# Low halves of 46 weight tiles: an accumulating DMA onto a negated copy in place of a VectorE subtraction

## The chip, the cores and the metric

The kernel runs on one core of one Trainium2 chip. The metric is device microseconds of one execution, lower being better. Three runs of the kernel before are shown (860.07, 862.01 and 861.69 us); their median is 861.69 us.

Engines are named as the profile names them: PE is TensorE (its weight loads are PEld), DVE is VectorE, ACT is ScalarE, POOL is GpSimd, and SP is the engine whose queue issues the kernel's DMAs.

## What is computed

One layer on a sequence of 512 rows of width 1024: a modulated standardisation, a mixer of two branches (an mLSTM with 4 heads and an S5 state-space branch with 32 groups), a layer norm, and a convolutional GLU feed-forward net with a hidden width of 2816. What matters here is the mixer, since the weights that the change touches are those of its input projection, its GLU and its down projection:

```python
proj = h @ w_in + b_in
xm, om, ip, fp, us, ga, gb = jnp.split(proj, IN_SPLITS, axis=-1)
...
y_a = (hm * mlstm_norm_gain * jax.nn.sigmoid(om)) @ w_mlstm_down
ys = jax.nn.gelu(_s5_ssm(us, ...))
val, gate = jnp.split(ys @ w_s5_glu, 2, axis=-1)
y_b = val * jax.nn.sigmoid(gate)
y = jax.nn.sigmoid(ga) * y_a + jax.nn.sigmoid(gb) * y_b
return y @ w_mix_out
```

All of it is float32. PE multiplies in the type float32r, which keeps fewer bits, so the kernel splits each operand into a high part (rounded to float32r) and a low part (what rounding left), and adds three products: high times high, high times low, low times high.

## The kernel before

Everything is tiled to 128 partitions. A weight tile `w` is 128 x 1024 float32 (512 KB): the eight 128 x 128 blocks that one output tile of 128 columns needs for its eight steps over the width of 1024. The SP queue loads it into one of two buffers `w`. ACT writes its rounded copy `wh` and DVE the difference `wl`, each into one of three buffers (`split_into`, L220 to L222; the DVE instruction stands on L210, in `sub`). PE then runs 8 times three matmuls of 512 columns (`mm3`, L241 to L244): L242 and L243 use `wh`, L244 uses `wl`.

46 such tiles go through a list, `todo` (L740 to L750): 30 of the input projection (`in_win`: the tiles x2 to x7, the eight o tiles and the sixteen g tiles), 8 of the GLU (`in_wglu`) and 8 of the down projection (`in_wdn`). `ahead` (L752) keeps a tile's pair one tile ahead of its use: with `PF = 1`, the split of tile i+1 is issued before the matmuls of tile i. With three buffers, the ACT copy of tile i+1 has to wait until PE has finished with tile i-2.

The order of the work is written by hand in the string `SEQ` (L144): tokens for the projection tiles (x, o, g), for steps of the S5 branch (S) and of the heads (H), for GLU and down tiles (l, d), and for steps of a second modulation product (A), which streams 256 KB pieces of `in_wa` through buffers `hh` and adds them up on DVE (L202, `s5h<-hh,k,s5h`). A scheduler of the framework then orders each engine's instructions by its own estimate, so that matmuls of projection tiles fill PE between the steps of heads and S5. In time, the kernel falls into these stretches: start and the eight k steps (the first of the 46 tiles is split at 57 us), projection tiles between heads and S5 (to 305 us; 26 of the 46 are split there), gate, GLU and down tiles back to back (305 to 428 us; the other 20, with A steps beside them), mix output and layer norm (428 to some 500 us), and the feed-forward net to the end.

POOL does small things: masks of the heads (`affine_select`, L854), the scaling of the o tiles (L786), inverse square roots (L278, L279), memsets. It issues no DMA.

Of the kernel before, what the change touches and what calls it, by code (L numbers as in the profile page):

```python
# [10 lines left out]
F32R = mybir.dt.float32r  # L11
I32 = mybir.dt.int32
AF = mybir.ActivationFunctionType
ALU = mybir.AluOpType
# [144 lines left out]
def _build(ctx, tc, nc, h):  # L159
    V, A, T, GP = nc.vector, nc.scalar, nc.tensor, nc.gpsimd  # L160
# [4 lines left out]
    def tl(tag, shape, dt=F32, bufs=None, pool=None):  # L165
        uid[0] += 1
        return (pool or sb).tile(list(shape), dt, tag=tag, name=f"{tag}_{uid[0]}", bufs=bufs or BUFS[tag])
# [11 lines left out]
    def big(shape=(P, D), dt=F32, tag="hb"):  # L179
        return tl(tag, shape, dt)  # L180
# [10 lines left out]
    def dma(o, i):  # L191
        return nc.sync.dma_start(o, i)  # L192
# [16 lines left out]
    def sub(o, a, b):  # L209
        V.tensor_tensor(o, a, b, op=ALU.subtract)  # L210

    def f32(ap):
        return ap.bitcast(F32)

    def wload(ap, n=D, tag="w"):
        w = big(tag=tag)
        dma(w[:, :n], ap)
        return w

    def split_into(hi, lo, x):  # L220
        A.copy(hi, x)  # L221
        sub(lo, x, f32(hi))  # L222

    def wsplit(ap, n=D, tags=("wh", "wl"), w=None):
        w = wload(ap, n) if w is None else w
        wh, wl = (big(dt=F32R, tag=t) for t in tags)
        split_into(wh[:, :n], wl[:, :n], w[:, :n])
        return wh, wl

    def new_pair(tag):  # L230
# [494 lines left out]
    def kstep(j):  # L725
        wc = nxt[1]
        if j < KD - 1:
            nxt[:] = wa_load(j + 1), w0_load(j + 1)
        w0h, w0l = wsplit(None, NXM0 * P, w=wc)
        if j < KD - 1:  # L730
            pend = ada1_mm(j + 1, nxt[0])
        for m in range(NXM0):
            if j < KD - 1 and m == M1:
                ada1_cols(j + 1, *pend)
            if j < KD - 1 and m == M2:
                htr(j + 1)
            sl = slice(m * P, (m + 1) * P)
            mm3(acc0[m], w0h[:, sl], w0l[:, sl], hp[j][0], hp[j][1], j == 0, j == KD - 1)

    todo, ready = [], []  # L740
# [10 lines left out]

    def ahead():  # L752
        while todo and len(ready) <= PF:
            ready.append(wsplit(todo.pop(0)))
        return ready.pop(0)

    def proj(m):
        if m < NXM0:
            return acc0[m]
        wh, wl = ahead()  # L760
        o = acc()
        for k in range(KD):
            sl = slice(k * P, (k + 1) * P)
            mm3(o, wh[:, sl], wl[:, sl], hp[k][0], hp[k][1], k == 0, k == KD - 1)
        return o
# [187 lines left out]
    def glu_tile(j):  # L953
        wh, wl = ahead()
        pvl, pgt = bank("hd"), bank("hd")
        for i, o in ((1, pgt), (0, pvl)):
            for k in range(4):
                sl = slice((4 * i + k) * P, (4 * i + k + 1) * P)
                mm3(o, wh[:, sl], wl[:, sl], ys[k][0], ys[k][1], k == 0, k == 3)
        b = hh()  # L960
        A.activation(b, pgt, AF.Tanh, scale=0.25)
        stt(b, b, 1.0, pvl, ALU.add, ALU.mult)
        stt(gab[j][:, 1], gab[j][:, 1], 1.0, b, ALU.add, ALU.mult)

    def down_tile(j):
        wh, wl = ahead()
        pa = acc()
        for k in range(KD):
            sl = slice(k * P, (k + 1) * P)
            mm3(pa, wh[:, sl], wl[:, sl], hmg[k][0], hmg[k][1], k == 0, k == KD - 1)  # L970
        a = hh()
        stt(a, gab[j][:, 0], 1.0, pa, ALU.add, ALU.mult)
        stt(a, gab[j][:, 1], 0.5, a)
        yp.append(pair_of(a, "hb" if j < 5 else "s5b" if j < 7 else "s5h"))
# [218 lines left out]
    def val_half(j, gg, ov):  # L1193
        tt(gg, ov, gg)
        gp_.append(pair_of(gg, "hp" if j < 8 else "hb" if j < 13 else "s5b" if j < 15 else "hx" if j < 18 else "gab"))

    early = [(u, wsplit(h["wup"][u], tags=("wh", "wl") if i < 3 else ("hb", "hb")), bank("hd"))
             for i, u in enumerate((1, 0, 3, 2)[:NS])]
    for hv in range(2):
# [10 lines left out]
    for j in range(NF):  # L1210
# [5 lines left out]
        for u in (2 * j + 1, 2 * j):  # L1216
            if u in pre:
                ou[u] = pre[u]
            else:
                w = wsplit(h["wup"][u])  # L1220
# [36 lines left out]
```

## Time and profile before

| | |
|---|---|
| three runs | 860.07, 862.01, 861.69 us; median 861.69 |
| profiled execution: span from first to last instruction | 862.0 us |
| PE, PEld busy | 828.5 us (96%), 669.2 us (78%) |
| DVE busy | 607.1 us (70%) |
| ACT busy | 368.6 us (43%) |
| POOL busy | 98.0 us (11%) |
| mean granted TensorE clock | 0.994 |
| DMA | 105.94 MB, mean 123 GB/s; HBM read 101.01 MB |

The profiled execution has no other time than its span, which lies within the three runs and 0.3 us above their median. Busy times are sums over the whole span, and a stage's own limit has to be read in that stage. Matmuls overlap in the records (one of 512 columns is shown as 0.39 to 0.40 us, and the next begins some 0.23 us after it), so a PE that is busy throughout can still hide small bubbles; idle time of PE is certain, busy time is not all work.

### The profile page before, as it was taken

The page shows a single profiled execution, that of the slowest core. Times are in us where ns is not written, and L with a number is a line of the kernel's source. Part 1 is how long each engine was busy: PE and PEld are TensorE (multiplying, and loading weights), DVE is VectorE, ACT ScalarE, POOL GpSimd, SP SyncE. Part 2 cuts the span into 40 slices and gives each one's busy share as a digit, 9 for nine tenths or more (in the row PEclk, how much of TensorE's full clock was granted, in tenths as well). Part 3 has the DMA queues.
Part 4 walks back from the last instruction along what each step waited for, and adds up shares of the span by engine and source line. Part 5 has one row for each costly group of instructions (what it writes and reads, how often), then busy time and mean ns, then how long its engine had stood idle before and what let it go on. Part 6 is the DMA issues. An engine that isn't in the chain of part 4 may idle for free.

```text
span 862.0 us, 11353 instructions
## 1 busy us (share of the span) xinstructions
PE 828.5 (96%) x4106; PEld 669.2 (78%) x4106; DVE 607.1 (70%) x1144; ACT 368.6 (43%) x589; POOL 98.0 (11%) x255
## 2 busy tenths in 40 slices
PE   3999999999999999999999999999999999999996
PEld 1777868778777778888887988888888878888785
DVE  5557978788689774578978767556777675878144
ACT  4454573564556442232334555444444444333000
POOL 2781211122022100000002200000000000000000
PEclk9999999999999999999999999999999999999998
DMA  9832132122222233568655023224444232445011
GB/s 336 288 132 86 53 101 62 45 85 62 79 60 87 86 123 122 196 203 294 210 191 177 2 74 102 94 98 147 146 147 137 86 120 74 171 163 169 11 49 49
DMA packets 45415, 105.94 MB, mean 123 GB/s; under 512 B 13360, under 2 KB 14256, under 8 KB 45360
## 3 DMA queue, kind: packets, MB, share of 16 engines
q1 hardware_dynamic: 45360, 105.23, 36.0%
q8 instruction: 32, 0.52, 0.2%
q14 instruction: 23, 0.19, 0.1%
HBM read 101.01 MB, written 2.10 MB: 120 GB/s over the span
## 4 chain that ended last, share of the span: by engine, by line
PE 76%; DVE 11%; ACT 4%; DMA 4%; issue 2%; SPq 2%; POOL 0%; DVEq 0%; ACTq 0%; POOLq 0%
PE acc L242 11%; PE acc L243 11%; PE acc L244 11%; PE hd L242 11%; PE hd L243 11%; PE hd L244 11%; DVE hh L202 2%; SPq L192 2%; DVE s5h L207 1%; PE s L242 1%; PE s L244 1%; PE s L243 1%; DVE wl L210 1%; PE s L612 1%; DMA w<-in_wmix 1%
## 5 line engine op out<-in xcount | busy, mean ns | idle before, releaser
L221 ACT CAST wh<-w 128x1024 fp32r<-128x1024 f32 (+2 forms) x103 | 103.2, 1003 | 144.0 <-PE acc L243 111.5
L210 DVE TENSOR_TENSOR wl<-w,wh 128x1024 fp32r<-128x1024 f32 (+2 forms) x103 | 120.5, 1172 | 60.8 <-ACT wh L221 60.1
L242 PE MATMUL acc<-hp,wh 128*128 128x512 f32 x256 | 103.4, 405 | 0.5 <-ACT hx L785 0.5
L244 PE MATMUL acc<-hp,wl 128*128 128x512 f32 x256 | 102.1, 399 | 0.0
L243 PE MATMUL acc<-hp,wh 128*128 128x512 f32 x256 | 102.1, 399 | 0.0
L242 PE MATMUL hd<-s5b,wh 128*128 128x512 f32 (+1 forms) x168 | 63.4, 380 | 0.7 <-ACT s5b L1169 0.5
L243 PE MATMUL hd<-s5b,wh 128*128 128x512 f32 (+1 forms) x168 | 63.6, 379 | 0.2 <-DVE s5b L210 0.2
L244 PE MATMUL hd<-s5b,wl 128*128 128x512 f32 (+1 forms) x168 | 63.3, 378 | 0.0
L242 PEld LDWEIGHTS acc<-hp,wh 128*128 128x128 f32 x256 | 48.2, 189 | 14.7 <-issue 3.7
L202 DVE SCALAR_TENSOR_TENSOR hh<-hh,hh 128x512 f32<-128x512 f32 x52 | 35.9, 691 | 31.2 <-ACT hh L564 14.7
L244 PEld LDWEIGHTS acc<-hp,wl 128*128 128x128 f32 x256 | 48.4, 189 | 11.2 <-issue 0.4
L243 PEld LDWEIGHTS acc<-hp,wh 128*128 128x128 f32 x256 | 48.4, 189 | 10.8 <-issue 0.4
L202 DVE SCALAR_TENSOR_TENSOR s5h<-hh,k,s5h 128x512 f32<-128x512 f32 x56 | 39.3, 746 | 4.7 <-DMA hh<-in_wa 4.6
L242 PEld LDWEIGHTS hd<-s5b,wh 128*128 128x128 f32 x168 | 31.3, 188 | 7.6 <-ACT s5b L1169 0.8
L243 PEld LDWEIGHTS hd<-s5b,wh 128*128 128x128 f32 x168 | 31.7, 189 | 7.0 <-DVE s5b L210 0.6
L244 PEld LDWEIGHTS hd<-s5b,wl 128*128 128x128 f32 x168 | 31.6, 188 | 6.4
L202 DVE SCALAR_TENSOR_TENSOR hh<-hh,k,hh 128x512 f32<-128x512 f32 x44 | 33.0, 751 | 4.5 <-ACT hh L1186 3.6
L1024 POOL TENSOR_SCALAR mov<-mov 128x1 f32<-128x1 f32 x6 | 3.7, 624 | 276.2 <-ACT s L1023 159.6
L244 PE MATMUL acc<-hx,wl 128*128 128x512 f32 x84 | 33.1, 394 | 0.0
L242 PE MATMUL acc<-hx,wh 128*128 128x512 f32 x84 | 33.1, 394 | 0.0
L243 PE MATMUL acc<-hx,wh 128*128 128x512 f32 x84 | 33.1, 394 | 0.0
L244 PE MATMUL acc<-s5b,wl 128*128 128x512 f32 x80 | 31.6, 395 | 0.5 <-DVE wl L210 0.5
(547 smaller groups left out, 2053.1 us busy)
## 6 DMA issues: line engine op xcount, KB each, us to landing
w<-in_wup SPq DMA_DIRECT2D x44, 512.0 KB, 3.2
hh<-in_wa SPq DMA_DIRECT2D x64, 256.0 KB, 4.2
w<-in_win SPq DMA_DIRECT2D x30, 512.0 KB, 3.2
w<-in_wfd SPq DMA_DIRECT2D x22, 512.0 KB, 3.3
hb<-in_wa SPq DMA_DIRECT2D x16, 512.0 KB, 7.4
w<-in_wglu SPq DMA_DIRECT2D x8, 512.0 KB, 3.3
w<-in_wdn SPq DMA_DIRECT2D x8, 512.0 KB, 3.3
w<-in_wmix SPq DMA_DIRECT2D x8, 512.0 KB, 4.2
```

The costliest lines, as they stand in the source:

```text
L192: return nc.sync.dma_start(o, i)
L202: V.scalar_tensor_tensor(o, i0, s, i1, op0=op0, op1=op1)
L207: V.tensor_tensor(o, a, b, op=op)
L210: V.tensor_tensor(o, a, b, op=ALU.subtract)
L221: A.copy(hi, x)
L242: T.matmul(o, lhsT=wh, rhs=xh, start=first, stop=False)
L243: T.matmul(o, lhsT=wh, rhs=xl, start=False, stop=False)
L244: T.matmul(o, lhsT=wl, rhs=xh, start=False, stop=last)
L612: T.matmul(o, lhsT=F[:, ri, pr, :], rhs=XB[:, ri, pr].rearrange("p g k -> p (g k)"), start=ri == 0, stop=False)
L1024: GP.tensor_scalar(v[:, 2:3], v[:, 0:1], v[:, 1:2], EPS * D, op0=ALU.add, op1=ALU.add)
```

## The change

For these 46 tiles DVE no longer subtracts. ACT still writes `wh`, and then writes minus `wh` into `wl`; POOL issues a DMA that reads the same 512 KB of the weight from HBM a second time and adds it, in flight, to what stands in `wl`. The sum is w minus wh, the same low half. The SP load of `w` stays, since `wh` is made from it. Buffers and `PF` are as before. The other splits (the first 8 steps' weights, the mix, feed-forward up and down weights, all activations) still go through DVE.

```diff
@@ -227,6 +227,14 @@
         split_into(wh[:, :n], wl[:, :n], w[:, :n])
         return wh, wl
 
+    def wsplit_dma(ap):
+        w = wload(ap)
+        wh, wl = (big(dt=F32R, tag=t) for t in ("wh", "wl"))
+        A.copy(wh, w)
+        A.activation(wl, f32(wh), AF.Copy, scale=-1.0)
+        GP.dma_start(wl, ap, accum_op=ALU.add)
+        return wh, wl
+
     def new_pair(tag):
         if tag in ("hx", "hh", "s5h"):
             return tl(tag, [P, 516], F32R)[:, :512], tl(tag, [P, 516], F32R)[:, :512]
@@ -751,7 +759,7 @@
 
     def ahead():
         while todo and len(ready) <= PF:
-            ready.append(wsplit(todo.pop(0)))
+            ready.append(wsplit_dma(todo.pop(0)))
         return ready.pop(0)
 
     def proj(m):
```

Lines of the changed kernel below the new function are 8 higher (L795 becomes L803). The scheduler also moves instructions. Three places follow. Names are tile names with a running number, output before the arrow.

First, DVE between the end of head 0 and the S5 step that follows (L207 on `s5h` is the S5 rotation). Before:

```order
L210 TENSOR_TENSOR wl_1772<-w_1769,wh_1771 128x1024
L207 TENSOR_TENSOR hh_1740<-hd_1735,hx_1192 128x512
L207 TENSOR_TENSOR hh_1751<-hd_1746,hx_1451 128x512
L210 TENSOR_TENSOR wl_1818<-w_1815,wh_1817 128x1024
L210 TENSOR_TENSOR hx_1743<-hh_1740,hx_1742 128x512
L202 SCALAR_TENSOR_TENSOR hh_1757<-hx_1009,k_61,hh_1757 128x512
```

and now:

```order
L207 TENSOR_TENSOR hh_1749<-hd_1744,hx_1195 128x512
L207 TENSOR_TENSOR hh_1760<-hd_1755,hx_1456 128x512
L210 TENSOR_TENSOR hx_1752<-hh_1749,hx_1751 128x512
L202 SCALAR_TENSOR_TENSOR hh_1766<-hx_1011,k_61,hh_1766 128x512
L210 TENSOR_TENSOR hx_1763<-hh_1760,hx_1762 128x512
```

The two subtractions into `wl` are gone from between the head's own steps; the rest keeps its order.

Second, ACT among gate tiles of the stretch from 305 to 428 us (L795, now L803, evicts a gate tile from PSUM; L961, now L969, a GLU tile's). Before:

```order
L221 CAST wh_3629<-w_3627 128x1024
L795 ACTIVATE gab_3555<-acc_3562,k_95 128x512
L221 CAST wh_3671<-w_3669 128x1024
L795 ACTIVATE gab_3594<-acc_3601,k_95 128x512
L961 ACTIVATE hh_3659<-hd_3634 128x512
```

and now:

```order
L233 CAST wh_3661<-w_3659 128x1024
L803 ACTIVATE gab_3585<-acc_3593,k_95 128x512
L234 ACTIVATE wl_3662<-wh_3661 128x1024
L233 CAST wh_3704<-w_3702 128x1024
L803 ACTIVATE gab_3625<-acc_3633,k_95 128x512
L234 ACTIVATE wl_3705<-wh_3704 128x1024
L969 ACTIVATE hh_3692<-hd_3667 128x512
```

Each copy into `wh` is now followed by the negation into `wl` (L234), here with one eviction between the two.

Third, POOL at the four masks of head 0 (`affine_select`, L854, now L862). Before:

```order
L786 TENSOR_SCALAR hx_1451<-hx_1451,k_61 128x512
L854 AFFINE_SELECT hh_1445<-hh_1445 128x128
L854 AFFINE_SELECT hh_1536<-hh_1536 128x128
L854 AFFINE_SELECT hh_1550<-hh_1550 128x128
L854 AFFINE_SELECT hh_1566<-hh_1566 128x128
```

and now:

```order
L794 TENSOR_SCALAR hx_1456<-hx_1456,k_61 128x512
L235 DMA wl_1679<-in_win 128x1024
L862 AFFINE_SELECT hh_1450<-hh_1450 128x128
L862 AFFINE_SELECT hh_1543<-hh_1543 128x128
L235 DMA wl_1713<-in_win 128x1024
L862 AFFINE_SELECT hh_1557<-hh_1557 128x128
L862 AFFINE_SELECT hh_1573<-hh_1573 128x128
```

POOL's queue now holds the DMA issues (L235) of the eighth and ninth of the 46 tiles, each of which waits for the ACT negation of its tile, ahead of masks that the head waits for.

## Rows read from the trace of the kernel before

**Rows 1.** The page, its line of engines: busy us, share, instructions.
```profile
PE 828.5 (96%) x4106; PEld 669.2 (78%) x4106; DVE 607.1 (70%) x1144; ACT 368.6 (43%) x589; POOL 98.0 (11%) x255
```

**Rows 2.** Engines' busy us by stretch: length, instructions, then clock, DMA share, GB/s.
```profile
57.00:305.00 248.00, 239.53 (x1326) 192.21 (x1326) 199.63 (x451) 133.24 (x232) 47.82 (x101) 0.99 0.23 72
305.00:375.00 70.00, 70.00 (x302) 56.45 (x301) 41.98 (x55) 23.62 (x31) 0.00 (x0) 1.00 0.45 151
375.00:428.00 53.00, 53.00 (x229) 42.82 (x228) 45.62 (x68) 16.13 (x23) 0.00 (x0) 1.00 0.75 253
428.00:455.00 27.00, 27.00 (x134) 22.45 (x133) 22.57 (x42) 9.92 (x17) 0.00 (x0) 1.00 0.54 185
```

**Rows 3.** Waits of PE, 57 to 305 us: us in total, times, longest.
```profile
PE s L612 <- DVE k L210: 3.3, 3, 1.7
PE hd L891 <- DVE hh L198: 1.8, 3, 1.0
```

**Rows 4.** Chain that ended last, pieces in time order: start us, us, what.
```profile
95.96 1.13 DVE wl L210
...
145.35 1.54 DVE wl L210
...
203.80 1.13 DVE wl L210
...
244.96 1.06 ACT wh L221
246.04 1.23 DVE wl L210
...
266.41 1.22 DVE wl L210
...
274.53 1.05 ACT wh L221
...
438.96 3.95 DMA w<-in_wmix
```

**Rows 5.** Groups by shape, 57 to 428 us: count | busy us, mean ns | idle before.
```profile
L210 DVE TENSOR_TENSOR wl<-w,wh 128x1024 fp32r<-128x1024 f32 x46 | 56.3, 1227 | 12.3 <-ACT wh L221 11.6 <-PE acc L244 0.4 <-issue 0.3
...
L221 ACT CAST wh<-w 128x1024 fp32r<-128x1024 f32 x46 | 48.2, 1047 | 80.3 <-PE acc L243 64.1 <-issue 9.5 <-PE hd L243 5.7
...
L795 ACT ACTIVATE gab<-acc,k 128x512 f32<-128x512 f32 x16 | 11.0, 685 | 0.8 <-DVE hh L202 0.6
```

**Rows 6.** The same groups: ACT over all, POOL from 57 to 330, ACT from 372 to 428.
```profile
L304 ACT ACTIVATE gab<-gab,nb,rs 128x1024 f32<-128x1024 f32 x4 | 4.6, 1228 | 7.0 <-DVE nb L202 7.0
...
L786 POOL TENSOR_SCALAR hx<-hx,k 128x512 f32<-128x512 f32 x8 | 9.8, 1228 | 40.2 <-ACT hx L785 40.1
L854 POOL TENSOR_SCALAR_AFFINE_SELECT hh<-hh 128x128 f32<-128x128 f32 x16 | 7.1, 445 | 71.3 <-ACT hh L853 69.9 <-issue 1.3
...
L221 ACT CAST wh<-w 128x1024 fp32r<-128x1024 f32 x8 | 8.4, 1048 | 16.1 <-PE acc L243 10.5 <-issue 5.5
```

**Rows 7.** Timeline at 355 to 372 us: start us, us, instruction [idle before <-releaser].
```profile
354.98 1.05 ACT L221 CAST wh<-w 128x1024 fp32r<-128x1024 f32 x1 [4.54 <-PE acc L243]
...
360.58 1.05 ACT L221 CAST wh<-w 128x1024 fp32r<-128x1024 f32 x1 [3.96 <-PE acc L243]
...
366.62 0.40 PE L244 MATMUL hd<-s5b,wl 128*128 128x512 f32 x1
...
371.53 0.39 PE L244 MATMUL hd<-s5b,wl 128*128 128x512 f32 x1
```

**Rows 8.** DMA queue (MB, share of 16 engines), and issues: KB each, us to landing.
```profile
q1 hardware_dynamic: 45360, 105.23, 36.0%
...
w<-in_wdn SPq DMA_DIRECT2D x8, 512.0 KB, 3.3
```

**Rows 9.** DMA issues from 386 to 399 us, and the issuing instruction there.
```profile
w<-in_win SPq DMA_DIRECT2D x1, 512.0 KB, 5.8
...
L192 SPq DMA_DIRECT2D w<-in_win x1: 327/327/327, 387.2 to 387.2; - x1
```

## The prediction

> **What bounds the kernel now.** I read the page's line of engines first, then the table of stretches, PE's waits, the chain that ended last, and the timeline and DMA issues where the tiles run densest. PE is busy for 96% of the span and DVE for 70% [rows 1], so DVE's work is worth time only where PE waits for it. The table of stretches [rows 2] says where that can be. From 57 to 305 us, where projection tiles fill PE between heads and S5, PE is busy 239.5 of 248 us, DVE 199.6 (80%): 8.5 us are open. From 305 to 428 us PE is busy for every microsecond, so nothing can be won there. What is scarce there instead are the DMA engines: their share is 0.45 to 375 us and 0.75 from there to 428. PE's waits [rows 3] put 3.3 + 1.8 = 5.1 us of the open 8.5 on DVE. The chain [rows 4] shows five of the subtractions that the change removes lying on it, and, later, loads of the mix weights. The granted clock is 0.99 to 1.00 in all these stretches [rows 2], so no term hangs on it.
>
> **What is removed.** 46 DVE subtractions of 1.227 us, 56.3 us in all [rows 5]. 26 of them lie before 305 us. The five on the chain took 1.13 + 1.54 + 1.13 + 1.23 + 1.22 = 6.25 us [rows 4]; PE cannot get back more than it waits for, so the gain is at most 5.1 us, and at least nothing, since the scheduler also moves what waits for DVE. The 20 after 305 us are worth nothing: PE hides them all. I take the whole 5.1 as the gain, because the subtractions lie right on the chain, and charge what replaces them against it.
>
> **What is added on ACT.** 46 negations of 128x1024. No such row exists; the copy of that shape takes 1.047 us [rows 5], an activation of that shape with per-partition scale and bias 1.228 us [rows 6]. The negation has a constant scale, so I take 1.05 us, 48 us in all, 27 of them before 305 us on an ACT that is busy 133 of 248 us [rows 2]. Mostly PE's other tiles cover them. On the chain two copies into `wh` stand as ACT pieces [rows 4], and a negation stands right behind or near each copy now, so I charge two times 1.05 = 2.1 us (bounds: 0, if neither stays on the chain, and the whole gain of 5.1). First stretch: -5.1 + 2.1 = **-3.0 us** (bounds -5.1 and 0).
>
> **What is added on POOL.** 46 DMA issues. SP's issue takes 0.33 us [rows 9], a POOL pass over 128x512 takes 1.228 us [rows 6]; no row shows POOL issuing a transfer, and I take the upper one, 1.2 us, the pass of its own engine. That is 55 us on an engine that is nearly idle after 305 us. Before 305 us the issues stand among the masks of the heads, 16 of 0.445 us that already wait for ACT [rows 6]. An issue that waits for its negation holds back the masks behind it, and a head's DVE and PE steps wait for those; but the negation of that tile waits for PE to end a tile three earlier, and by the order of the program the head's matmuls come after that too. I charge nothing: projection tiles stand between on PE. Without that cover each held mask would cost about the path of copy, negation and issue, 3.3 us.
>
> **Whether the low half comes in time.** Between 305 and 428 us a tile's copy starts when PE ends the tile three before (354.98 us), and PE wants its low half at 366.62 us, 11.6 us later; tiles follow each other every 5.6 us [rows 7]. The new path in it: copy 1.05, an eviction of 0.685 that stands between [rows 5], negation 1.05, POOL 1.2: 4.0 us until the transfer is on its way, and 7.6 us left for it. A plain load of 512 KB lands in 3.3 us [rows 8] when little else runs, and in 5.8 us between 386 and 399 us [rows 9]. The accumulating one also has to read `wl` out of SBUF before it writes it, so its price lies between one plain load and two in a row: 3.3 to 6.6 us undisturbed, 5.8 to 11.6 us in the crowd. I take the upper price undisturbed (6.6, a microsecond to spare: no cost to 375 us). In the crowd 5.8 is in time and 11.6 is 4.0 us late; I take the middle, 8.7, which is about 1 us late. Lateness is shared by three buffers, so a tile pays a third of it: 8 tiles [rows 6] times 0.35 = 2.8 us.
>
> **Whether the DMA engines have room.** All loads of before took 36.0% of 16 engines' span for 105.23 MB [rows 8]: 310 us, so 512 KB (0.524 MB) cost 1.55 us of all 16 engines. Bounds for the accumulating transfer are 1.55 and twice that, 3.1 us; since two operands go in for one that comes out, I take 3.1. From 375 to 428 us the old loads need 0.75 x 53 = 39.8 us. Eight of the tiles are split from 372 us on [rows 6], so 8 x 3.1 = 24.8 us come on top: 64.6 us of work for 53 us, 11.6 us too much (at 1.55 it would be 52.2, and fit). The next stretch, to 455 us, is used for 0.54, so by 439 us, where the load of a mix weight stands on the chain [rows 4], 0.46 x 11 = 5.1 us of the arrears are worked off and 6.5 are left. If PE is 2.8 us slower already, so much more time was there for the DMAs; what is late at the mix weights is then 6.5 - 2.8 = 3.7 us. Both together: **+6.5 us** (bounds 0 and 11.6).
>
> By the Trainium skill, "DMA: Bandwidth & Descriptors", section "Issuing engines are not separate DMA queues", transfers issued by SP and by POOL run on the same 16 engines and interleave; no row here shows it, since all data of before went through q1. By that rule the sum above stands, and with engines of their own for POOL's transfers it would be the fast rival below. The Trainium skill, "Collectives: The Full Stack", section "The bandwidth ceiling: the fold count and why AG ≠ RS ≠ AR", says that an add in the DMA engines is free, while its second source read halves the rate (measured 1.93 times); by that an estimate for one transfer is 3.0 us, and the sum would be 0.8 us lower. It speaks against this change, and no run here shows it yet.
>
> Other edits: the second read of the weights adds 46 x 0.524 = 24 MB of HBM reads, already counted as DMA time. `w` comes free after the copy and not after the subtraction, so SP may issue its next load a microsecond or two earlier; with the engines full this moves the queue, not the work, and I cost it at nothing.
>
> **Sum.** 862.0 (the profiled span; the runs' median is 0.3 lower) - 3.0 + 6.5 = 865.5, less the 0.3 to stand against the median: **865 us**, 0.4% slower than 861.69. A measurement of this kernel can tell about 0.2% (1.7 us) from no change.
>
> **Rivals.**
> - *The DMAs fit* (chance 0.30). If the accumulating transfer costs the engines 1.55 us, 375 to 428 us needs 52.2 of 53 us and nothing is late; 861.7 - 3.0 = 858.7 us, faster. For it: before 305 us the engines are far from full (0.23 [rows 2]). Against: it moves more than a plain load.
> - *It cancels* (0.22). A price of 2.1 to 2.4 us per transfer leaves 3.6 to 6.0 us of arrears at 428, of which 0 to 0.9 is left at 439, and 1 to 3 us of late tiles remain against the gain; or the negations eat the gain: 861.7 us, within 1.7.
> - *Every dense tile is late* (0.12). If a transfer lands after 11.6 us in the whole of 305 to 428, each of 20 tiles is 4.0 us late and pays 1.3: +27 us, some 885 us. It decides from a landing of 7.6 us on; each microsecond over that costs 20/3 = 6.7 us.
> - *POOL's queue holds the heads back* (0.03). Four heads times 3.3 us, less the gain: 872 us.
>
> **Chances.** The forecast has 0.33. Slower by over 0.2%: 0.33 + 0.12 + 0.03 = 0.48; within: 0.22; faster: 0.30. The range starts at 856 us, the full gain of 5.1 with a little over, and ends at 880, a landing of about 10.8 us in all dense tiles (3.2 late, 21 us, less 3.0); beyond it I leave some 0.15.
>
> **What would show it.** Right: DVE busy about 551 us, ACT about 417, POOL up by 40 to 60; a second DMA queue with 24 MB; DMA share near 1 between 375 and 428 us; a POOL transfer landing after 6 to 9 us; PE waiting for a DMA into `wl` at L252 and later for the mix weights; PE's waits for DVE before 305 us down from 5.1 to 1 or 2 us. Wrong on the fast side: landings under 7.6 us throughout and no PE wait on `wl`. Wrong on the slow side: waits on `wl` at nearly every tile from 305 us, or masks of heads waiting behind a POOL issue.

## The result and the profile after

The changed kernel took 889.1 us (median of four runs, 886.44 to 892.36) against 861.7 us before: ratio 1.0323, 95% interval 1.0302 to 1.0343. It is slower by 27 us; 865 us were forecast, with a range of 856 to 880. Of all the runs below one was slow (e2, 922.95 us at a granted clock of 0.849), and e2's median is that of its other three.

The page of the changed kernel, engines and DMA queues (they answer to [rows 1, 8]):

```profile
PE 833.4 (94%) x4106; PEld 670.4 (76%) x4106; DVE 559.0 (63%) x1098; ACT 411.5 (46%) x635; POOL 134.5 (15%) x301
...
q1 hardware_dynamic: 45360, 105.23, 35.2%
q0 software_dynamic: 6624, 24.12, 15.8%
...
wl<-in_wglu POOLq DMA_DIRECT2D x8, 512.0 KB, 7.6
```

DVE lost 48 us of work and PE none, and still the end is later. The second queue took 15.8% of 16 engines over a span of 886.4 us: 140 us, or 3.04 us for each of the 46 transfers. The stretches (columns as in [rows 2]):

```profile
57.00:305.00 248.00, 235.67 (x1303) 189.06 (x1304) 170.41 (x423) 152.66 (x254) 64.64 (x125) 0.99 0.55 125
305.00:375.00 70.00, 66.33 (x283) 52.47 (x282) 25.49 (x37) 33.45 (x39) 10.33 (x12) 1.00 0.86 216
375.00:428.00 53.00, 42.63 (x177) 33.68 (x176) 25.77 (x40) 19.96 (x24) 6.33 (x8) 0.90 0.93 256
428.00:455.00 27.00, 24.88 (x114) 19.55 (x113) 18.25 (x29) 10.38 (x15) 1.74 (x2) 1.00 0.83 244
```

Against [rows 2], PE was busy 3.9 us less before 305 us, and from 375 to 428 us, where it had been busy throughout, 10.4 us less. In that stretch the DMA share rose from 0.75 to 0.93, but the rate hardly did (253 to 256 GB/s): the engines worked more for the same bytes.

To see where time is lost I follow PE's progress: the start of its last matmul before the first of the 46 tiles, of the last of the 24th tile, and of the last of the 46th, in the timelines. Before:

```profile
70.79 0.39 PE L244 MATMUL hd<-hp,wl 128*128 128x512 f32 x1
...
304.55 0.39 PE L244 MATMUL hd<-s5b,wl 128*128 128x512 f32 x1
...
428.25 0.40 PE L244 MATMUL acc<-hx,wl 128*128 128x512 f32 x1
```

The changed kernel:

```profile
69.54 0.40 PE L252 MATMUL hd<-hp,wl 128*128 128x512 f32 x1
...
311.11 0.39 PE L252 MATMUL acc<-hp,wl 128*128 128x512 f32 x1
...
452.96 0.39 PE L252 MATMUL acc<-hx,wl 128*128 128x512 f32 x1
```

The delay is -1.25, then +6.56, then +24.71 us: **+7.8 us over the first 24 tiles and +18.1 over the other 22**. Behind tile 46 nothing is added (both need some 433 us more). The start of an execution wanders: at 70 us the kernels below stand between -2.9 and +2.0. So I use the two differences, here called first part and dense part, and read nothing below 2 us. They come from the one profiled execution of each run, which lies up to 3.4 us from the run's median.

The scheduler gave PE another order too: the changed kernel's 4106 matmuls stand in another order than before in 64 places. Runs e2, e4, e9, e11 and e12 below have exactly the changed kernel's order on PE, and e3 that of the kernel before.

PE's waits, 57 to 305 us (compare [rows 3]):

```profile
PE hd L250 <- ACT hb L221: 4.9, 2, 4.2
PE s L620 <- DVE k L210: 2.2, 3, 1.1
PE hd L250 <- ACT hb L844: 1.7, 1, 1.7
PE hd L899 <- DVE hh L198: 1.4, 2, 0.7
```

and from 305 to 455 us, where there were none:

```profile
PE acc L252 <- DMA wl<-in_wdn: 12.9, 4, 9.4
PE hd L250 <- ACT s5b L221: 1.2, 1, 1.2
```

DVE's two lines fell from 5.1 to 3.6 us, and waits for ACT (before 305 us) and for DMAs (behind it) took more than their place. Both long waits (4.2 and 9.4 us) are the end of something that began elsewhere. The second one, in the timelines of SP, DVE, ACT, POOL and PE, in order of time:

```profile
382.83 22.26 SPq L192 DMA_DIRECT2D hh<-in_wa  x12
...
392.15 0.49 DVE L196 TENSOR_SCALAR s5h<-hh,k 128x512 f32<-128x512 f32 x1 [9.34 <-DMA hh<-in_wa]
...
404.00 3.40 DVE L202 SCALAR_TENSOR_TENSOR s5h<-hh,k,s5h 128x512 f32<-128x512 f32 x5 [3.95 <-DMA hh<-in_wa]
...
405.15 0.90 SPq L192 DMA_DIRECT2D w<-in_wdn  x1
...
405.49 0.60 ACT L969 ACTIVATE hh<-hd 128x512 f32<-128x512 f32 x1 [9.58 <-DVE s5h L202]
410.19 1.04 ACT L233 CAST wh<-w 128x1024 fp32r<-128x1024 f32 x1 [4.10 <-DMA w<-in_wdn]
411.26 1.06 ACT L234 ACTIVATE wl<-wh 128x1024 fp32r<-128x1024 f32 x1
...
412.61 0.87 POOL L235 DMA_DIRECT2D wl<-in_wdn  x1 [15.49 <-ACT wl L234]
...
421.40 0.80 PE L252 MATMUL acc<-hx,wl 128*128 128x512 f32 x1 [9.39 <-DMA wl<-in_wdn]
422.00 0.63 PE L250 MATMUL acc<-hx,wh 128*128 128x512 f32 x1
```

An `in_wa` load lands late and the A step on DVE waits 9.3 us. SP needs 22 us to get rid of twelve `in_wa` issues, which share seven `hh` buffers, and the next down weight stands behind them until 405.15. SP's own wait for landings, 380 to 410 us, and the landings of `in_wa` from 375 to 428 us, before and now:

```profile
SPq L192 <- DMA hh<-in_wa: 13.9, 3, 8.9
```
```profile
hh<-in_wa SPq DMA_DIRECT2D x31, 256.0 KB, 4.3
```
```profile
hh<-in_wa SPq DMA_DIRECT2D x27, 256.0 KB, 5.6
```

The first of the twelve took 8.9 us to land. ACT's GLU eviction wants an `hh` buffer too, and waits 9.6 us. The copy of the weight then waits for its load, the negation for the copy, POOL for the negation, and PE for the landing, some 8 us after POOL's issue ended. PE shows its wait at `wl`, but the first thing late in this chain was a load that the change did not touch.

### The profile page after: what moved, and what is told of

Same layout as the page of the kernel before. It is cut to its first block, busy times and chain, and to the rows that moved or that the text cites. A ratio compares the mean times of both kernels' runs of the same rounds, so it can differ in the third digit from the quotient of the medians.

```text
span 886.4 us, 11447 instructions
## 1 busy us (share of the span) xinstructions
PE 833.4 (94%) x4106; PEld 670.4 (76%) x4106; DVE 559.0 (63%) x1098; ACT 411.5 (46%) x635; POOL 134.5 (15%) x301
## 3 DMA queue, kind: packets, MB, share of 16 engines
q0 software_dynamic: 6624, 24.12, 15.8%
## 4 chain that ended last, share of the span: by engine, by line
PE 70%; DVE 11%; DMA 10%; issue 4%; ACT 4%; SPq 1%; POOL 1%; DVEq 0%; ACTq 0%; POOLq 0%
PE hd L250 10%; PE acc L250 10%; PE hd L252 10%; PE acc L252 10%; PE hd L251 10%; PE acc L251 10%; DMA hh<-in_wa 4%; DVE hh L202 3%; DVE s5h L207 2%; DMA w<-in_wdn 2%; PE s L250 2%; PE s L252 2%; PE s L251 2%; DMA wl<-in_wdn 1%; DMA wl<-in_win 1%
## 5 line engine op out<-in xcount | busy, mean ns | idle before, releaser
L210 DVE TENSOR_TENSOR wl<-w,wh 128x1024 fp32r<-128x1024 f32 (+2 forms) x57 | 64.3, 1129 | 48.6 <-ACT wh L221 48.6
L233 ACT CAST wh<-w 128x1024 fp32r<-128x1024 f32 x46 | 48.1, 1046 | 77.8 <-PE acc L251 50.8
L221 ACT CAST wh<-w 128x1024 fp32r<-128x1024 f32 (+2 forms) x57 | 54.9, 968 | 61.9 <-PE acc L251 44.9
L234 ACT ACTIVATE wl<-wh 128x1024 fp32r<-128x1024 f32 x46 | 48.6, 1057 | 0.6
L235 POOL DMA_DIRECT2D wl<-in_win x30 | 26.7, 889 | 112.4 <-ACT wl L234 88.3
L210 DVE TENSOR_TENSOR hb<-hh,hb 128x512 fp32r<-128x512 f32 (+3 forms) x42 | 25.8, 617 | 20.1 <-ACT hb L221 20.0
L1191 POOL MEMSET hh<- 128x2 f32 x22 | 2.2, 99 | 225.9 <-DVE hh L202 106.4
```

What stands on the lines that cost most here:

```text
L233: A.copy(wh, w)
L234: A.activation(wl, f32(wh), AF.Copy, scale=-1.0)
L235: GP.dma_start(wl, ap, accum_op=ALU.add)
L1191: GP.memset(gb_[:, 0:2], 0.0)
```

## The experiments

Diffs are against the changed kernel, unless it says otherwise. This table has what came out; ratios are against the kernel before in the same series. The times of e3 to e6, e9, e11 and e12 came out inside the range of a theory that had been written down, e2's a microsecond above it, e1's and g12's in that of a rival (g12's by a loss that neither had expected), and those of e7, e8, e10 and g11 above every range.

| run | median us | ratio, 95% interval | first part | dense part |
|---|---|---|---|---|
| changed kernel | 889.1 | 1.0323 (1.0302 to 1.0343) | +7.8 | +18.1 |
| e1 negate on ACT, add on DVE | 868.01 | 1.0070 (1.0045 to 1.0096) | +6.2 | 0.0 |
| e2 first 25 tiles only | 870.05 | 1.0098 (1.0072 to 1.0123) | +8.4 | -0.1 |
| e3 last 21 tiles only | 882.42 | 1.0225 (1.0199 to 1.0251) | +0.1 | +20.2 |
| e4 plain DMA | 871.76 | 1.0110 (1.0081 to 1.0140) | +3.2 | +9.4 |
| e5 half of `in_wa` | 874.08 | 1.0142 (1.0108 to 1.0177) | +7.0 | +5.8 |
| e6 before, half of `in_wa` | 861.16 | 0.9989 (0.9976 to 1.0002) | -1.7 | 0.0 |
| e7 low half not read | 894.45 | 1.0374 (1.0317 to 1.0431) | +8.6 | +6.2 |
| e8 negate on DVE | 894.19 | 1.0387 (1.0340 to 1.0435) | +7.0 | +24.6 |
| e9 no DMA | 864.21 | 1.0034 (1.0016 to 1.0053) | +0.1 | 0.0 |
| e10 negate on POOL | 905.64 | 1.0498 (1.0475 to 1.0521) | +28.5 | +14.8 |
| g11 subtract on POOL, 25 tiles | 907.17 | 1.0514 (1.0489 to 1.0538) | +45.1 | 0.0 |
| g12 subtract on POOL, 46 tiles | 920.24 | 1.0669 (1.0647 to 1.0691) | +42.3 | +1.8 |
| e11 a sixteenth of the bytes | 864.72 | 1.0029 (1.0017 to 1.0041) | 0.0 | +2.0 |
| e12 weights from POOL's queue | 893.69 | 1.0353 (1.0331 to 1.0375) | +8.1 | +20.2 |

### e1 to e4: which half, and which part

e1 keeps the negation and lets DVE add; e2 and e3 use the new split for one half of the tiles; e4 copies in place of adding:

```diff
-        GP.dma_start(wl, ap, accum_op=ALU.add)
+        tt(wl, w, f32(wl), ALU.add)
```
```diff
-            ready.append(wsplit_dma(todo.pop(0)))
+            nth[0] += 1
+            ready.append((wsplit_dma if nth[0] <= 25 else wsplit)(todo.pop(0)))
```
```diff
-        GP.dma_start(wl, ap, accum_op=ALU.add)
+        GP.dma_start(wl, ap)
```

(e3 has `nth[0] > 25` in the second.)

> The 46 negations stay on ACT, and DVE adds w to them; POOL issues no DMA. Theory (the DMA engines are oversubscribed): the loss of 27 us goes, 861 to 866 us, the few us being ACT's 46 x 1.05 us among the heads. Rival (the negations stand in ACT's way): the 6 us that were lost by the end of the 25th tile stay, 868 us or more.

> The first 25 of the 46 tiles (all that are split before the GLU and down stretch) by the accumulating DMA, the other 21 by DVE. Theory: only the loss of the first stretch stays, +5 to +7 us, 867 to 869 us, and PE is never held at a low half after 305 us. Rival (the loss in the dense stretch comes from what the first stretch left late): 880 us or more.

> The first 25 tiles by DVE, the last 21 by the accumulating DMA. Theory: the loss of the dense stretch alone, +16 to +21 us, 878 to 883 us, with loads of in_wa landing late and PE held once for about 10 us at a down tile. Rival (as in the run with the first 25): under 868 us.

> POOL's DMA only copies, it does not add (the low half then holds the whole weight). Same issues, same waits, same bytes from HBM. Theory (engine time of the transfer): a copy costs half the engine time, about 1.55 us of 16 engines in place of 3.05, the work of 375 to 428 us fits again, and at most a third of the loss stays, 862 to 872 us. Rival (POOL's issue and the landing of a second load as such): 882 us or more.

The two halves add up: 7.7 + 20.0 us of medians against 27. Either half can be looked at alone. e4's queue, and its stretch from 375 to 428 us:

```profile
q0 software_dynamic: 6624, 24.12, 8.9%
...
375.00:428.00 53.00, 47.30 (x190) 37.38 (x189) 29.97 (x47) 20.11 (x24) 4.30 (x8) 0.94 0.89 301
```

Of a span of 872.7 us that is 1.69 us per transfer; the adding one costs 1.8 times as much. The stretch moved 301 GB/s at a lower share, so the 256 GB/s of the changed kernel were not the most that could be read from HBM there; that leaves the engines' time. With copies alone the dense part still lost 9.4 us in the profiled execution (the slowest of four, 2.8 us above the median), although by that price the work of the prediction's sum all but fits (53.3 of 53 us).

e1's first part lost 6.2 us with no transfer at all. From it I concluded at first that ACT's negations cost some 5 us there. That fell with e9, which has the negations and not DVE's 46 passes, and loses 0.1: where nothing is transferred, the 6.2 us come only with 46 passes on ACT and on DVE. The order on PE also differs between e1 and e9, so they are not taken apart further.

### e5, e6: fewer other bytes

In both kernels the second half of each A step reuses the first half's tile.

```diff
-                wi = hh()
-                dma(wi, h["wa2"][kc, :, q * D + i * 512:q * D + (i + 1) * 512])
+                if i == 0:
+                    wi = hh()
+                    dma(wi, h["wa2"][kc, :, q * D + i * 512:q * D + (i + 1) * 512])
```

> The changed kernel with half of the in_wa loads left out: the second half of each step of that stage reuses the tile of the first half, so the output differs. Instructions on PE, DVE, ACT and POOL stay as they are. Theory (too many bytes in 305 to 455 us, so that loads come late one behind the other): with the DMA share of 0.93 in 375 to 428 us falling to 0.75 or below, the loss behind 305 us of 18 us falls below 6, and the kernel takes 868 to 875 us. Rival (what counts is the longer way of each low half from its cast to its landing, whatever else the DMA engines do): landings fall from 7.4 us to some 6 at most, three or four waits at the low half stay, and it takes 880 us or more.

> The kernel before with the same half of the in_wa loads left out, as the partner of the run above; the output differs. Both theories: PE is the bound there and these loads are hidden, so 860 to 863 us. If it were below 858, the loads cost something in the kernel before too, and the run above has to be read against this one.

The dense part falls from 18.1 to 5.8 us while every accumulating DMA is still there, and the kernel before doesn't care (0.9989). The DMA share from 375 to 428 us did not fall as I expected; work that had been late moved up. The stretch 375 to 428 us of e5:

```profile
375.00:428.00 53.00, 51.21 (x221) 41.13 (x220) 32.84 (x52) 25.49 (x33) 7.88 (x9) 1.00 0.96 257
```

PE is busy 51.2 us there, at a share of 0.96: nearly full DMA engines alone did not hold PE up here. In 428 to 455 us e5 uses 0.56, the changed kernel 0.83.

### e7: nobody waits for the landing

```diff
-        return wh, wl
+        return wh, wh
```

> The changed kernel with every accumulating DMA still issued, but the low half left out of the products: the third group of matmuls of a tile reads the high half again, so that PE never waits for a landing and the output differs. Theory (late loads of in_wa and of weights, made so by the bytes): the waits move to other tiles, most of the loss stays, 878 to 888 us. Rival (the wait at the landing is the loss): only the 5 us of the negations stay, 866 to 873 us.

894.45 us: taking away the wait at the low half recovers nothing. Up to tile 46 the dense part is down to +6.2, but the A steps behind it were as late as ever, and PE met that later, in waits that the changed kernel did not have (timeline of e7):

```profile
448.84 1.05 PE L996 MATMUL s<-k,hx 128*128 128x2 f32 x8 [3.38 <-DVE hx L210]
...
453.16 0.37 PE L996 MATMUL s<-k,hx 128*128 128x2 f32 x1 [2.12 <-ACT hx L221]
```

Behind tile 46 it lost 11.2 us more, 5.5 of them in these two waits and most of the rest at a granted clock of 0.75 from 448 to 475 us (0.25 x 27 = 6.8 us at most). So the rival of the landing falls, and e5 and e7 together say: what is lost in the dense part goes with the transfers' time on the DMA engines, wherever PE meets it.

### e8, e9: engines without bytes

e8 negates with `ts(wl, f32(wh), -1.0)` on DVE in place of `A.activation`; e9 drops the DMA:

```diff
-        GP.dma_start(wl, ap, accum_op=ALU.add)
```

> The changed kernel with the negation as a DVE multiplication by -1 in place of the ACT activation, and the accumulating DMA as it is. Theory (the first stretch loses some 5 us because ACT, which casts the heads and weights one after the other, carries the negations): the delay at tile 24 falls from 6.6 us to between 0 and 3, the dense loss stays, in all 880 to 886 us. Rival (the delay of the first stretch is from the DMAs' crowding of small loads): the delay at tile 24 stays at 6 or more, 887 to 892 us.

> The changed kernel without its accumulating DMAs: ACT casts and negates as before, DVE stays relieved of the 46 subtractions, and the low half of these tiles is left at minus the high half, so the output differs. It shows what the work on the engines does without one byte more. Theory A (the first stretch loses because ACT, which the heads wait for, carries 46 negations): the delay at tile 24 is 3 to 5 us, in all 864 to 868 us. Theory B (all of the loss comes from the transfers; the forecast of -3.0 us for the first stretch holds where there are none): 857 to 860 us, and no wait of PE at a low half.

e8's first part stays at +7.0 with ACT relieved, and e9's is +0.1 with ACT burdened: the first part's loss is not that of ACT's negations. (e8 alone could not say so, since its negations load DVE in ACT's place; its dense part, +24.6, was not taken apart.) e9's median fell into theory A's range of 864 to 868 us, but its delay at tile 24 is -2.4 us, not 3 to 5. The first part isn't the gain of theory B either. PE's waits of e9 from 57 to 305 us:

```profile
PE s L619 <- DVE k L210: 2.0, 3, 1.1
PE hd L249 <- ACT hb L221: 1.9, 2, 1.5
PE hd L898 <- DVE hh L198: 1.4, 2, 0.7
PE acc L249 <- ACT hx L792: 0.8, 1, 0.8
```

DVE's two lines fell by 1.7 us, from 5.1 to 3.4, and the lines on ACT, with three of 0.6 to 0.7 below these, came to 4.6 us, against 2.9 us in the same view of the kernel before. The relief and the negations cancel. At tile 46 the profiled e9 stood 2.45 us ahead, all of it from its start; its span ended 2.3 us behind (864.3 against 862.0). The 4.8 us between went in 428 to 455 us, where the granted clock was 0.81 (0.19 x 27 = 5.1 us):

```profile
428.00:455.00 27.00, 26.64 (x102) 21.67 (x103) 19.89 (x36) 10.73 (x17) 0.00 (x0) 0.81 0.53 178
```

Its twelve runs fall into two groups by their mean granted clock: seven at 0.997 to 0.998 took 861.93 to 864.24 us, and five at 0.989 to 0.992, the profiled one among them, 866.22 to 869.26 us. Without the drop e9 is about a microsecond slower than the kernel before (862.97 against 861.92 us).

### e10, g11, g12: POOL does the elementwise work

e10 negates on POOL ahead of the DMA; g11 and g12 are the kernel before with POOL's subtraction for 25 or all 46 tiles:

```diff
-        A.activation(wl, f32(wh), AF.Copy, scale=-1.0)
+        GP.tensor_scalar(wl, f32(wh), -1.0, None, op0=ALU.mult)
```
```diff
-        split_into(wh[:, :n], wl[:, :n], w[:, :n])
+        A.copy(wh, w)
+        GP.tensor_tensor(wl, w, f32(wh), op=ALU.subtract)
```

> The changed kernel with the negation on POOL, ahead of the DMA that POOL issues; ACT has no instruction more than in the kernel before, DVE none of the 46 subtractions. Theory A (ACT's queue costs the first stretch some 5 us): the delay at tile 24 falls below 3 us, and the dense stretch loses 15 to 22 us as in the changed kernel: 876 to 886 us. Theory B (the transfers cost both stretches): the delay at tile 24 stays at 4 us or more, in all 884 to 895 us.

> The kernel before with the subtraction of the first 25 of the 46 tiles on POOL in place of DVE; no negation and no DMA. POOL takes 1228 ns for 128x512 with one input in the kernel before, so a tile takes an estimated 2.5 to 5 us there. Theory B (DVE's relief is worth some 3 us in 57 to 305 us if nothing comes in its place): 857 to 861 us, if POOL's small instructions for the heads are not held back. Theory A (any longer way of the low half or any load on an engine that the heads wait for costs as much): 863 to 870 us.

> The kernel before with all 46 subtractions on POOL, no DMA. Partner of the run with the negation on POOL: that one differs by the transfers alone (a negation and a DMA in place of a subtraction). Theory of the transfers: the dense stretch loses 0 to 2 us here, since a tile takes 5.6 us of PE there and POOL has nothing else: 857 to 866 us. Rival (any longer way from the cast to the low half is lost in the dense stretch): each of 16 tiles there adds its POOL time beyond DVE's 1.23 us, 880 us or more.

The group of POOL's subtractions in g12:

```profile
L234 POOL TENSOR_TENSOR wl<-w,wh 128x1024 fp32r<-128x1024 f32 x46 | 116.5, 2533 | 162.2 <-ACT wh L233 129.7
```

and of its negations in e10:

```profile
L234 POOL TENSOR_SCALAR wl<-wh 128x1024 fp32r<-128x1024 f32 x46 | 136.5, 2968 | 127.1 <-ACT wh L233 127.0
```

In the first part all three lose 28 to 45 us, far more than expected. In g11 and g12 the traces show one reason: DVE is often held while POOL subtracts. Of g12's DVE instructions 34 took over 1.5 us, 84.2 us in all, and each of the 34 overlaps a subtraction on POOL; in the kernel before there is one of over 1.5 us. Two lines of g12's timelines (the DVE form takes 0.7 us elsewhere):

```profile
443.62 5.20 POOL L234 TENSOR_TENSOR wl<-w,wh 128x1024 fp32r<-128x1024 f32 x2 [4.67 <-ACT wh L233]
...
444.10 2.47 DVE L210 TENSOR_TENSOR hb<-hh,hb 128x512 fp32r<-128x512 f32 x1 [1.16 <-ACT hb L221]
```

e10, whose POOL pass has one operand, has only four such instructions; what held its heads up stays open.

The dense part is what they were for. There g12's low half comes 1.3 us later after its copy than DVE's (2.53 against 1.23), and the loss is +1.8; e10, also late and with transfers, loses 14.8. A longer way costs little up to tile 46, where 11.6 us are there for it. But g12 lost 12.4 us more behind tile 46, in PE's waits for what follows the A steps (5.0 us) and at a granted clock of 0.72 from 470 to 500 us (0.28 x 30 = 8.4 us at most). And since POOL's subtraction holds DVE and its negation hardly does, e10 and g12 do not differ by the transfers alone. That the transfers cost the dense part rests on e9 and e11 (0.0 and +2.0), not on this pair. No version with POOL beats the kernel before.

### e11: all issues, a sixteenth of the bytes

```diff
-        GP.dma_start(wl, ap, accum_op=ALU.add)
+        GP.dma_start(wl[:, :64], ap[:, :64], accum_op=ALU.add)
```

> The changed kernel with each accumulating DMA cut to 64 of the 1024 columns: 46 issues on POOL with the same waits in front of them, a sixteenth of the bytes; the low half is w minus wh in these columns and minus wh in the others, so the output differs. Theory (the bytes cost the first stretch, by making other loads late): the delay at tile 24 is between -3 and 0 us as in the run without DMAs, in all 861 to 867 us. Rival (POOL's queue, in which the heads' masks stand behind the issues): the delay at tile 24 stays at 3 us or more, 867 us or more.

```profile
q0 software_dynamic: 6624, 1.51, 2.0%
```

The first part is 0.0 with all 46 issues on POOL, the same number of packets (6624), the same waits ahead of them and the same order on PE: it is the bytes. How they act there shows at one place, the first head at 104 to 117 us, in the timelines of DVE, ACT and PE. e11:

```profile
110.09 0.75 DVE L202 SCALAR_TENSOR_TENSOR s5h<-hx,k,s5h 128x512 f32<-128x512 f32 x1 [1.77 <-DMA s5h<-s5h]
...
110.88 0.63 ACT L570 ACTIVATE s5h<-s5h 128x512 f32<-128x512 f32 x1 [2.67 <-DVE s5h L202]
...
113.76 0.50 PE L250 MATMUL hd<-hb,hb 128*128 128x512 f32 x1 [1.23 <-ACT hb L221]
```

The changed kernel:

```profile
113.13 0.75 DVE L202 SCALAR_TENSOR_TENSOR s5h<-hx,k,s5h 128x512 f32<-128x512 f32 x1 [4.97 <-DMA s5h<-s5h]
...
113.92 0.63 ACT L570 ACTIVATE s5h<-s5h 128x512 f32<-128x512 f32 x1 [5.86 <-DVE s5h L202]
...
116.57 0.50 PE L250 MATMUL hd<-hb,hb 128*128 128x512 f32 x1 [4.20 <-ACT hb L221]
```

The same instructions, one behind the other: DVE's wait for a 32 KB transfer of the S5 branch is 3.2 us longer, ACT's wait for DVE 3.2 us, PE's wait for the head's cast, which stands behind on ACT, 3.0 us. With plain copies (e4) DVE's wait here is 3.52 us, between the two. The DMA issues from 57 to 305 us, e11 and then the changed kernel:

```profile
s5h<-hx SPq DMA_DIRECT2D x32, 32.0 KB, 2.1
```
```profile
s5h<-hx SPq DMA_DIRECT2D x32, 32.0 KB, 3.4
```

This half of the branch's small transfers lands in 3.4 us in place of 2.1 beside the transfers of 512 KB, at a mean share of only 0.55. The other half (`s5h<-s5h`) keeps its median of 2.1 us, but single ones come late, as the one that DVE waits for above. This place accounts for 3 of the 7.8 us. Another 3.6 us more than e11 go at the last head, behind 271 us, where the granted clock was 0.94 from 276 to 305 us against e11's 1.00 (0.06 x 29 = 1.7 us at most); the rest there was not taken apart.

### e12: past SP's queue

```diff
-        w = wload(ap)
+        w = big(tag="w")
+        (GP if by_pool else nc.sync).dma_start(w, ap)
```

(`by_pool` holds for the last 21 tiles.)

> The changed kernel with the plain load of the weight of the last 21 of the 46 tiles issued on POOL's queue, ahead of its accumulating DMA, in place of SP's. Bytes and instructions stay. Theory A (SP's queue in order: the weight's load is late since it stands behind in_wa loads that wait for buffers): the delay at tile 42 falls from 21.7 us to 15 or less, in all 876 to 884 us. Theory B (the bytes don't fit into 375 to 428 us, in whatever order they are issued): in_wa loads or landings are late instead, 885 to 895 us.

Theory B: 893.69 us. The delay at tile 42 is 16.5 us, less than 21.7 but not 15 (from each one's own start 19.0 against 22.9), and tiles 43 to 46 lose another 9 us. SP's twelve `in_wa` issues took nearly as long without the weights between them (18.9 against 22.3 us), and PE's long wait is there (timeline of e12):

```profile
396.10 18.85 SPq L192 DMA_DIRECT2D hh<-in_wa  x12
...
415.48 0.79 PE L253 MATMUL acc<-hx,wl 128*128 128x512 f32 x1 [7.63 <-DMA wl<-in_wdn]
```

SP's order moved what is paid from one tile to others and did not lower it.

## Why the prediction was wrong

**The cause in one line.** The loss follows the time that the transfers take on the 16 DMA engines. By price per transfer (q0's share times the span over 46): 0.38 us (e11, 2.0% of 863.0) lost 0.0 + 2.0 us in the two parts, 1.69 us (e4) 3.2 + 9.4, and 3.04 us 7.8 + 18.1. Without transfers (e9) it is 0.1 + 0.0. Against the forecast's terms the dense part was 11.6 us dearer (18.1 for 6.5) and the first part 10.8 (7.8 for -3.0). The order on PE is the same in all four runs, so the reordering is not the cause. The transfers are not the only thing that can cost the first part: e1 lost 6.2 us there without one, with both DVE and ACT loaded, which the changed kernel does not do.

**"Whether the DMA engines have room": the step that failed.** The price of a transfer was right (3.1 taken, 3.04 measured), and so was the sign. What failed is the sum behind it. It treated the engines as a store of time: 64.6 us of work for 53, arrears of 11.6, 5.1 worked off by 439 us, 6.5 left for PE to meet at the mix weights. Measured: 18.1 us, over the upper bound of 11.6 as well, 12 of them at tile 42 (the delay there rises from 9.5 to 21.7), well ahead of the mix weights. Three things were left out. The arrears fall on what is in flight at the time, and here on `in_wa` loads, which no line of the prediction followed. Those share buffers `hh` with ACT's GLU eviction and stand on one SP queue with the weights, so that one late load made DVE, ACT, the copy, the negation and POOL late in turn. And while the chain waits, the work that would fill the engines isn't issued: the share was 0.93, not 1. e4 shows that the form of the sum, not a size, was at fault: 1.69 us is near the 1.55 at which I wrote that it would fit (8 x 1.69 + 39.8 = 53.3 of 53 us; rival "The DMAs fit", 858.7 us), and it lost 9.4 us in the dense part of its profiled execution, 6.6 if all that this execution was above the median fell there.

**"-5.1 + 2.1 = -3.0": failed twice.** Of the 5.1 us that PE waits for DVE only 1.7 went (e9); I had taken all of it because subtractions lie on the chain, but the lines L612 and L891 end in DVE's other work on the S5 branch and the heads, which stayed. The negations took 1.7 back (charged: 2.1). So the engines' part is 0, the edge of the bounds that I gave; e1 and e9 say that both terms were larger than I took them, the relief of DVE beside the negations being worth 6.1 us (6.2 against 0.1). What was missing entirely is a term for the transfers before 305 us. The share there was 0.23, and I counted that as room; it became 0.55, and +7.8 us came with the transfers' bytes (0.0 with a sixteenth of them, e11), 3 of them seen through a small transfer that landed late on the path of the first head.

**"Whether the low half comes in time": nearly right, and beside the point.** Landings were 5.6 us over all `in_win` tiles and 7.4 to 7.6 in the GLU and down tiles; 8.7 was taken for the crowd, with 7.6 to spare. PE did wait at `wl`, six times behind 305 us and four of them at down tiles, but the longest wait came from a copy that was late, and without any wait at `wl` (e7) the kernel was no faster.

**Right.** Copy and negation (1.05 taken, 1.057 measured), DVE 551 (559), ACT 417 (411.5), the second queue's 24 MB. POOL rose by 36.5 us, a little less than the 40 to 60 named. POOL's issue took 0.88 us, not 1.2, and to charge nothing for it in the heads was right (e11).

**The two rules that were weighed.** That transfers from POOL and SP share the same 16 engines (the Trainium skill, "DMA: Bandwidth & Descriptors", "Issuing engines are not separate DMA queues"): the traces agree, since loads of SP's queue land later by what POOL's queue moves (3.4 against 2.1 us). That the second source read and not the add costs, 1.93 times (the Trainium skill, "Collectives: The Full Stack", "The bandwidth ceiling: the fold count and why AG ≠ RS ≠ AR"): here it was 3.04 / 1.69 = 1.80 times. That an adding transfer costs nearly double agrees; no run here separates the read from the add.

## What to carry to other kernels

Moving work from a busy engine onto DMA was paid here in time of the 16 engines, and an add onto SBUF counted nearly double (1.80 times); price it against the busiest stretch, and ask there which old load gets late and what shares its buffers and its queue. A low mean DMA share is no room: at 0.55, half of the small transfers on a serial path here already landed 60% later. Of the time that PE waits for an engine, count as gain only what is ended by the very instructions removed, not all waits that end on that engine. And before calling two runs partners, check in the traces that the engines' other work takes as long in both.

## What the runs showed of the hardware that was not expected

- An accumulating DMA of 512 KB took 3.04 us of all 16 engines, a plain copy of the same from the same queue 1.69 us, and SP's loads before 1.55 us ([rows 8], worked out in the prediction).
- On POOL, multiplying 128x1024 by -1 took 2968 ns (e10), more than subtracting two such tiles, 2533 ns (g12), though it reads one operand fewer. But the subtraction held DVE: 34 of DVE's instructions took over 1.5 us in g12 and 20 in g11, all of them beside one of POOL's subtractions, against four in e10 and one in the kernel before.
- Behind PE's wait of 9.39 us the granted clock was 0.63 from 412 to 426 us, and the matmul behind it shows 0.63 in place of 0.39 us. In e9 a wait of half a microsecond at 428.36 us preceded 0.81. Each such dip is a piece at 0.5 of the clock in a stretch at 1.00, here 10.2 us long in both. These dips are a small part of the loss: in the changed kernel 22 matmuls of 512 columns between 57 and 460 us began 0.43 us before the next in place of 0.23, 13 more than before, 0.19 us each, 2.5 us in all.
